# Padding SBUF slots by 32 bytes in a one-core decoder block (hybrid HGRN2 and sliding-window attention)

## The chip, the cores and the metric

One core of a Trainium2 chip runs the whole program. The metric is the device time of one execution in microseconds (us), the median of several. TensorE multiplies a stationary operand (the weights, loaded by an instruction of their own, LDWEIGHTS) with a moving operand (512 token columns at most); its granted clock has two levels, 1.2 and 2.4 GHz. In the profile PE is TensorE's matmul row, PEld its weight loads, DVE VectorE, ACT ScalarE, POOL GpSimd, SP SyncE.

## The reference, cut to what matters

One layer of a decoder block, on 512 tokens of width 2048, all in float32:

```
h = modulate(rms_norm(x, norm1_g), shift1, scale1)
proj = h @ w_in                       # 2048 -> 9728: HGRN2 q,f,i,g | attention q,k,v | two gates
o_hg = HGRN2 recurrence, chunkwise    # 8 heads of 128
o_at = sliding-window attention       # 16 heads of 64, window 128, sinks, relative bias
merged = sigmoid(gate_hg) * (o_hg @ w_branch_hg) + sigmoid(gate_at) * (o_at @ w_branch_attn)
x = x + gate1 * (merged @ w_out)
h2 = modulate(rms_norm(x, norm2_g), shift2, scale2)
x = x + gate2 * (square(relu(h2 @ w_ff1)) @ w_ff2)
```

The conditioning (shift, scale, gate) comes from another product, silu(c) @ w_ada.

## The kernel before, in words

All activations lie transposed, 128 channels on partitions by 512 tokens. A projection makes one tile of 128 output channels at a time: for each block of 128 input channels it multiplies a 128x128 piece of weights with the 512 token columns. To keep float32 accuracy with the faster one-pass float32r products, weights and activations are each split into a high part and a low part, and each block takes three products (function mm3): high weights times high activations, high weights times low activations, low weights times high activations. Each of the three is preceded by its own weight load, so the stream on TensorE is load, product, load, product, and the load for the next product runs while the present one streams.

The main stream is a list of items; an item is a piece of weights of 128 x 512 (four blocks, twelve products). Raw weights arrive by DMA from SP's queue into `raw` slots (3 of 4096 bytes a partition). `pump_splits` runs up to two items ahead: ScalarE copies a piece into a `whi` slot, VectorE writes the remainder into a `wlo` slot (4 slots each). The moving tiles come in pairs of neighbouring slots, high and low: `A` slots (32) hold the 16 pairs of the normalized input (later those of the merged branches and of the second norm), `O` slots (25) hold among others the eight pairs of a branch's output or of an eighth of the MLP's hidden layer, and in the first 190 us raw conditioning weights that DMAs write there. A planner in Python orders the side work (attention, HGRN2, conditioning) between the main products; its costs are constants and know nothing of addresses.

All these slots are 2048 bytes a partition, and come from one pool that lays tags out in the order of their first use: C, T, O, L, then 8 small slots `s` of 32 bytes and one `s16` of 64, then raw, whi, wlo, A and the rest. So within one tag all slots begin at the same offset modulo 2048; whi, wlo and A begin at one and the same offset, and O begins 320 bytes lower (8 x 32 + 64), which is 192 modulo 512. The 16 KB at the beginning of each partition are scratch for the descriptors of DMAs that GpSimd issues; after it and the slots some hundred bytes are left of the partition.

```
def mm3(ps, whi, wlo, x, first, last):
    mm(ps, whi, x[0], first, False)
    mm(ps, whi, x[1], False, False)
    mm(ps, wlo, x[0], False, last)
...
def take(tag, shape=None, dt=F32, name=None):
    pl.live[tag] = pl.live.get(tag, 0) + 1
    return act.tile(shape or [P, T], dt, tag=tag, bufs=BUFS[tag], name=nm(name or tag))
```

Of the kernel before, what the change touches and what calls it, by code (L numbers as in the profile page):

```python
# [11 lines left out]
F32R = mybir.dt.float32r  # L12
# [5 lines left out]
P = 128  # L18
T = 512
# [15 lines left out]
BUFS = {"A": 32, "O": 25, "C": 16, "T": 6, "L": 5, "ada": 3, "raw": 3, "whi": 4, "wlo": 4}  # L35


class Plan:
    """Keeps an estimate of each engine's time, and interleaves side work with the main stream of products."""

    def __init__(self):
        self.clk = {"PE": 0.0, "DVE": 0.0, "ACT": 0.0}
# [44 lines left out]
def tile_block(ctx, tc, xT, cT, wada1, wada2, badaT, g1T, g2T, wg0, win, wbat, wbhg, wout, wfg, wff1, wff2,  # L87
               lbT, hggT, qgT, kgT, sinks, table, ident_d, mask_d, onehot_d, neg_d, outT):
    nc = tc.nc
# [4 lines left out]
    act = ctx.enter_context(tc.tile_pool(name="act", bufs=1))  # L94
# [6 lines left out]
    def nm(s):  # L101
        uid[0] += 1
        return f"{s}_{uid[0]}"
# [4 lines left out]
            n *= s  # L108
        return n

# [1 line left out]
    def tt(out, in0, in1, op):  # L112
        nc.vector.tensor_tensor(out=out, in0=in0, in1=in1, op=op)  # L113
        pl.op("DVE", free_size(out) * 1.04 + 70)

    def stt(out, in0, scalar, in1, op0, op1):
        nc.vector.scalar_tensor_tensor(out=out, in0=in0, scalar=scalar, in1=in1, op0=op0, op1=op1)  # L117
        pl.op("DVE", free_size(out) * 1.04 + 70)

    def ts(out, in0, s1, op0, s2=None, op1=None):  # L120
        if op1 is None:
            nc.vector.tensor_scalar(out=out, in0=in0, scalar1=s1, scalar2=None, op0=op0)
        else:
            nc.vector.tensor_scalar(out=out, in0=in0, scalar1=s1, scalar2=s2, op0=op0, op1=op1)
        pl.op("DVE", free_size(out) * 0.6 + 70)
# [28 lines left out]
        PE.transpose(out=out, in_=in_, identity=ident)  # L154
        pl.op("PE", 107)

# [1 line left out]
    def take(tag, shape=None, dt=F32, name=None):  # L158
        pl.live[tag] = pl.live.get(tag, 0) + 1
        return act.tile(shape or [P, T], dt, tag=tag, bufs=BUFS[tag], name=nm(name or tag))  # L160

    def drop(tag, n=1):
# [17 lines left out]
    def small(n=4):  # L180
        return act.tile([P, n], F32, tag="s", bufs=8, name=nm("s"))

# [1 line left out]
    def cload(name, shape, src, dt=F32):  # L184
        t = cst.tile(shape, dt, name=name)
        G.dma_start(out=t, in_=src)
        return t
# [3 lines left out]
    for kt in range(KT):  # L191
        t = take("C")
# [18 lines left out]
    eps = cst.tile([P, 1], F32, name="eps")  # L211
# [3 lines left out]
    one = ones[:, 0:1]  # L215
# [20 lines left out]
    tt(c_act, c_sb, csig, ALU.mult)  # L236
    G.dma_start(out=cdram, in_=c_act)

# [1 line left out]
    def split(src, hi, lo):  # L240
        sact(hi, src, AF.Copy)
        tt(lo, src, hi.bitcast(F32), ALU.subtract)
# [4 lines left out]
        mm(ps, wlo, x[0], False, last)  # L247

    def newton(ps, s, y, w):
        """y * (1.5 - 0.5 (s ps + eps) y^2), with w = y^2."""  # L250
        stt(w, ps, EPS / s, w, ALU.add, ALU.mult)
        ts(w, w, -0.5 * s, ALU.mult, 1.5, ALU.add)
        tt(y, y, w, ALU.mult)
# [9 lines left out]
        for _ in gen:  # L263
            pass

# [1 line left out]
    items = []  # L267
    loads = []

    def add_load(src, n):  # L270
        loads.append((src, n))
        return len(loads) - 1
# [2 lines left out]
        items.append((ld, c0, w, emit, pre, post))  # L275

    def add_tile(srcs, xs, post, pre=None):
        """One tile of 128 output channels; xs() gives the (hi, lo) tiles of the moving side."""
        cell = {}
        nk = 8 * len(srcs)  # L280
        for hf, src in enumerate(srcs):
            ld = add_load(src, 1024)
            for q in range(2):
                k0 = hf * 8 + q * 4

                def emit(hi, lo, k0=k0):
                    x = xs(k0 + 4)
                    if k0 == 0:
                        cell["ps"] = acc()
                    for k in range(4):  # L290
                        mm3(cell["ps"], hi[:, k * P:(k + 1) * P], lo[:, k * P:(k + 1) * P], x[k0 + k], k0 + k == 0,
                            k0 + k == nk - 1)
                        if k == 1:
                            pl.drive()

                end = k0 + 4 == nk
                add_item(ld, q * T, T, emit, pre if k0 == 0 else None, (lambda: post(cell["ps"])) if end else None)
# [24 lines left out]
    def pump_splits(upto):  # L322
        while state["split"] < min(upto + 1, len(items)):
            ld, c0, w, *_ = items[state["split"]]
            hi = act.tile([P, w], F32R, tag="whi", bufs=BUFS["whi"], name=nm("whi"))
            lo = act.tile([P, w], F32R, tag="wlo", bufs=BUFS["wlo"], name=nm("wlo"))
            split(raws[ld][:, c0:c0 + w], hi, lo)
            wts[state["split"]] = (hi, lo)
            state["split"] += 1
# [13 lines left out]
        if drive:  # L343
            pl.drive()

# [1 line left out]
    def ada_step(a, raw, kt):  # L347
        if kt == 0:
            ts(a, raw, c_act[:, 0:1], ALU.mult)
# [8 lines left out]
        return act.tile([P, T], F32, tag="aa", bufs=1, name=nm("aa"))  # L358

    def ada_rest():  # L360
        """The other four parts: output channels on partitions, a quarter of the inputs at a time."""
        n = 0
        raw = []

        def fetch(n):
            while len(raw) < min(n + BUFS["ada"], 256):
                t = act.tile([P, T], F32, tag="ada", bufs=BUFS["ada"], name=nm("ada"))
                SP.dma_start(out=t, in_=wada2[len(raw)])
                raw.append(t)

        fetch(0)
        for g in range(4):
            for q in range(4):
                cb = ada_acc()
                SP.dma_start(out=cb, in_=bass.AP(cd.tensor, cd.offset + T * q, [[0, P], [1, T]]))
                lead = state["item"] + 2
                while state["item"] < lead:
                    yield "wait"
                for i in range(16):
                    fetch(n)  # L380
                    while state["item"] < n_start + PACE * n or 0 < len(mg) < KT:
                        yield "wait"
                    t = raw[n]
                    nc.vector.scalar_tensor_tensor(out=t, in0=t, scalar=1.0, in1=cb, op0=ALU.mult, op1=ALU.mult,  # L384
                                                   accum_out=adaq[:, i, q:q + 1])
                    pl.op("DVE", 680)
                    n += 1
                    yield
            d = slice(32 + 16 * g, 48 + 16 * g)
            t = adaq[:, :, 0]  # L390
            for q in range(1, 4):
                tt(t, t, adaq[:, :, q], ALU.add)
            tt(adaT[:, d], t, adaT[:, d], ALU.add)
            yield

# [1 line left out]
    h = []  # L397
    ev = {}

# [19 lines left out]
    sums = {}  # L419

    def start_evac(i, j, ps):
        """Tile i's products with the channel tiles 2j and 2j + 1 join its sum."""
        last = j == KT // 2 - 1
        key = skeys[i]
        if i in HELD:
            if not last:
                return
            src = ps
        else:
            if j == 0:  # L430
                sums[i] = take("O")
                sact(sums[i], ps, AF.Copy)
            else:
                tt(sums[i], ps, sums[i], ALU.add)
            drop("mx")
            src = sums[i]
        if last:
            if i < len(akeys):
                if i in HELD:
                    evac_to(key, "O", AF.Copy)(src)  # L440
                else:
                    ev[key] = src
                return
            if key[0] in ("q", "g"):
                evac_silu(key, "C")(src)
            else:
                evac_to(key, "C", AF.Copy if key[0] == "v" else AF.Sigmoid)(src)
            if i in HELD[NACC:]:
                drop("mx")
            elif i not in HELD:  # L450
                drop("O")
# [32 lines left out]
    for hd in range(NH):  # L484
# [3 lines left out]
        for kk in ("f", "q", "v", "g"):  # L488
            key = (kk, hd)
# [7 lines left out]
                add_tile(next_win(), hx, evac_silu(key, "C"))  # L497
    n_mix = len(items)

    # branches with their gates  # L500
    m = {}
    sig = {}
    xb = {0: [], 1: []}
# [63 lines left out]
                        msdone[n] = True  # L567
                add_tile([wb[n - SKEW[br]]], ready(xb[br]), post)

    # output projection  # L570
    x1 = []
    xr = {}
    sqs = {}
# [28 lines left out]
    for n in range(KT - 1):  # L602
        add_tile(halves(wout, n), ready(mg), out_post(n), xload(n))

    # the last tile of the projection and the first products of the MLP go by halves of the tokens,
    # so that the norm of one half runs under the products of the other
    HALF = [slice(0, T // 2), slice(T // 2, T)]
    h2 = []
    kept = []
# [168 lines left out]
    for g in range(8):  # L778
        for i in range(8):
            n = 8 * g + i  # L780
# [4 lines left out]
            add_tile([wff2[g, n]], ready(a_t[g]), ff2_post(g, n))  # L785
        items[a0 + 1], items[a0 + 2] = items[a0 + 2], items[a0 + 1]

# [1 line left out]
    def make_lb():  # L789
        mxl = small(8)  # L790
        tt(mxl, lbl[:, 0, :], lbl[:, 1, :], ALU.max)
# [126 lines left out]
        drop("T")  # L918
        drop("L")

# [1 line left out]
    oat = []  # L922

    def k_norm(raw):
# [50 lines left out]
        out.append(y)  # L975

    def att_unit(c, n, i, st):
        """Queries of block n: two heads of each of the chunk's two key heads, one in each half of the array."""
        qn, kn, vn, rq, bias, o = st["q"], st["k"], st["vn"], st["rq"][0], st["bias"], st["o"]
        rows = [slice(0, 64), slice(64, 128)]  # L980
        w = 128 if n == 0 else 256
# [47 lines left out]
        for half in range(nh):  # L1029
            t = take("L")  # L1030
# [67 lines left out]
        if c == 1:  # L1098
            yield from split_raw(oat, xb[0])

# [1 line left out]
    ohg = []  # L1102
    hgc = {}

# [167 lines left out]
        if hd == NH - 1:  # L1272
            drop("C", 3)

# [1 line left out]
    ctx.enter_context(tc.manual_schedule())  # L1276
    startup()
    assert state["item"] == n_start
# [104 lines left out]
```

## Time and profile before

| what | us |
|---|---|
| median of three runs | 2794.94 |
| lowest and highest of them | 2793.41, 3927.64 |
| span of the profiled execution | 2793.4 |
| PE busy in it (12630 products) | 2770.4 |
| DVE busy | 1305.8 |
| ACT busy | 932.3 |
| DMA queue of SP, share of 16 engines | 38.9% |

The profiled execution has a span of 2793.4 us, equal to the lowest run's 2793.41: nothing measurable lies around the span, and the median stands 1.5 us above it. Products are pipelined and overlap, so a product's own duration in the trace (about 390 ns) is not its cost; its cost is the distance from its start to the next one's start, called pace below.

### The profile page before, as it was taken

The numbers are of one execution on the slowest core, as the hardware profiler recorded it, in microseconds if no ns is written. First come the engines' busy times: TensorE is split into PE (matmuls) and PEld (weight loads), VectorE is DVE, ScalarE is ACT, GpSimd is POOL, SyncE is SP. The second block draws the span as 40 slices with busy tenths as digits, with TensorE's granted clock in tenths as the row PEclk, the third lists the DMA queues.
The fourth block names the chain that finished last, engine by engine and source line by source line (L and its number), as shares of the span: only waits on it lengthen the run. The fifth ranks groups of instructions, "written<-read, shape, count | busy, mean of one in ns | idle before, by whom it ended". The sixth has DMA issues, their size and how long they took to land.

```text
span 2793.4 us, 33013 instructions
## 1 busy us (share of the span) xinstructions
PE 2770.4 (99%) x12630; PEld 2225.1 (80%) x12630; DVE 1305.8 (47%) x2574; ACT 932.3 (33%) x1686; POOL 14.6 (1%) x28
## 2 busy tenths in 40 slices
PE   8999999999999999999999999999999999999999
PEld 4777777888888888888888888888888888888887
DVE  4778787655444555565543333233333323323333
ACT  4244455453222322232342332323323223232231
POOL 1000000000000000000000000000000000000000
PEclk9999999999999999999999999999999999999999
DMA  8852322434555555555223222222222222222233
GB/s 316 290 185 90 125 84 80 148 124 153 192 183 185 185 188 181 171 185 186 96 90 106 98 91 91 98 98 93 98 96 93 96 98 98 92 97 97 93 109 109
DMA packets 133791, 369.50 MB, mean 132 GB/s; under 512 B 15169, under 2 KB 15297, under 8 KB 133633
## 3 DMA queue, kind: packets, MB, share of 16 engines
q1 hardware_dynamic: 132480, 364.96, 38.9%
q0 software_dynamic: 1152, 2.43, 0.3%
q8 instruction: 99, 1.62, 0.3%
q14 instruction: 60, 0.48, 0.0%
HBM read 363.11 MB, written 4.23 MB: 131 GB/s over the span
## 4 chain that ended last, share of the span: by engine, by line
PE 97%; DVE 2%; ACT 1%; DMA 0%; issue 0%; SPq 0%; ACTq 0%
PE acc L150 87%; PE mx L150 9%; PE mx L154 1%; DMA C<-xT 0%; DVE wlo L113 0%; SPq L193 0%; DVE T L117 0%; DVE L L117 0%; DVE T L113 0%; ACT A L146 0%; ACT T L146 0%; ACT whi L146 0%; DVE s L999 0%; DVE C L117 0%; DVE A L117 0%
## 5 line engine op out<-in xcount | busy, mean ns | idle before, releaser
L150 PE MATMUL acc<-A,whi 128*128 128x512 f32 (+1 forms) x4608 | 1422.6, 390 | 2.5 <-ACT A L146 1.9
L150 PEld LDWEIGHTS acc<-A,whi 128*128 128x128 f32 x4608 | 858.1, 188 | 193.0 <-issue 9.0
L150 PE MATMUL acc<-A,wlo 128*128 128x512 f32 (+1 forms) x2304 | 894.7, 388 | 1.4 <-DVE wlo L113 1.4
L146 ACT ACTIVATE whi<-raw 128x512 fp32r<-128x512 f32 x944 | 570.0, 626 | 944.1 <-PE acc L150 879.1
L150 PE MATMUL acc<-O,whi 128*128 128x512 f32 x2560 | 803.0, 394 | 0.0
L113 DVE TENSOR_TENSOR wlo<-raw,whi 128x512 fp32r<-128x512 f32 x944 | 625.9, 686 | 357.1 <-ACT whi L146 355.6
L150 PEld LDWEIGHTS acc<-O,whi 128*128 128x128 f32 x2560 | 478.8, 187 | 118.1
L150 PEld LDWEIGHTS acc<-A,wlo 128*128 128x128 f32 x2304 | 433.1, 188 | 92.2 <-DVE wlo L113 2.2
L150 PE MATMUL acc<-O,wlo 128*128 128x512 f32 x1280 | 504.3, 394 | 0.0
L117 DVE SCALAR_TENSOR_TENSOR C<-acc,adaT,C 128x512 f32<-128x512 f32 x128 | 96.1, 751 | 453.0 <-PE acc L150 453.0
L150 PEld LDWEIGHTS acc<-O,wlo 128*128 128x128 f32 x1280 | 239.4, 187 | 59.2
L113 DVE TENSOR_TENSOR O<-T,O 128x512 fp32r<-128x512 f32 x64 | 44.4, 693 | 381.8 <-ACT O L146 381.8
L146 ACT ACTIVATE T<-acc 128x512 f32<-128x512 f32 x92 | 55.1, 598 | 460.3 <-PE acc L150 460.3
L384 DVE SCALAR_TENSOR_TENSOR ada<-ada,aa 128x512 f32<-128x512 f32 x256 | 175.6, 687 | 37.4 <-DMA ada<-wada 32.8
L150 PE MATMUL mx<-A,whi 128*128 128x512 f32 (+1 forms) x448 | 135.6, 385 | 2.4 <-ACT A L146 2.0
L150 PEld LDWEIGHTS mx<-A,whi 128*128 128x128 f32 x448 | 83.0, 193 | 24.2 <-issue 5.0
L150 PE MATMUL mx<-A,wlo 128*128 128x512 f32 (+1 forms) x224 | 84.9, 379 | 0.0
L146 ACT ACTIVATE T<-T 128x512 f32<-128x512 f32 (+1 forms) x102 | 62.6, 622 | 6.0 <-DVE T L113 3.4
L146 ACT ACTIVATE T<-C 128x512 f32<-128x512 f32 (+1 forms) x33 | 20.2, 617 | 94.9 <-DVE C L117 89.9
L150 PEld LDWEIGHTS mx<-A,wlo 128*128 128x128 f32 x224 | 43.2, 193 | 7.9
L113 DVE TENSOR_TENSOR O<-mx,O 128x512 f32<-128x512 f32 x56 | 37.9, 687 | 16.8 <-PE mx L150 15.8
L146 ACT ACTIVATE C<-acc 128x512 f32<-128x512 f32 x26 | 15.5, 598 | 86.7 <-PE acc L150 86.6
(155 smaller groups left out, 979.7 us busy)
## 6 DMA issues: line engine op xcount, KB each, us to landing
raw<-wff SPq DMA_DIRECT2D x248, 512.0 KB, 3.3
raw<-win SPq DMA_DIRECT2D x128, 512.0 KB, 3.7
ada<-wada SPq DMA_DIRECT2D x256, 256.0 KB, 4.0
O<-wada SPq DMA_DIRECT2D x128, 256.0 KB, 5.3
raw<-wout SPq DMA_DIRECT2D x32, 512.0 KB, 3.8
raw<-wg SPq DMA_DIRECT2D x24, 512.0 KB, 4.6
raw<-wbat SPq DMA_DIRECT2D x16, 512.0 KB, 3.4
raw<-wbhg SPq DMA_DIRECT2D x16, 512.0 KB, 3.5
```

Source lines behind the costliest of these rows:

```text
L113: nc.vector.tensor_tensor(out=out, in0=in0, in1=in1, op=op)
L117: nc.vector.scalar_tensor_tensor(out=out, in0=in0, scalar=scalar, in1=in1, op0=op0, op1=op1)
L146: nc.scalar.activation(out=out, in_=in_, func=func, **kw)
L150: PE.matmul(out, lhsT=lhsT, rhs=rhs, start=start, stop=stop)
L154: PE.transpose(out=out, in_=in_, identity=ident)
L384: nc.vector.scalar_tensor_tensor(out=t, in0=t, scalar=1.0, in1=cb, op0=ALU.mult, op1=ALU.mult, accum_out=adaq[:, i, q:q + 1])
```

## The change

Slots of `A`, `O`, `whi` and `wlo` become 2080 bytes instead of 2048; the tile used is the first 2048 bytes of its slot. Successive slots thus begin 32 bytes further on modulo 512. That needs 57 x 32 + 8 x 32 = 2080 bytes more a partition, for which the descriptor scratch of GpSimd's DMAs goes from its default of 16384 to 8192 bytes. Beside this, comments and docstrings are removed. No instruction is added or taken away.

```diff
     def take(tag, shape=None, dt=F32, name=None):
         pl.live[tag] = pl.live.get(tag, 0) + 1
+        if tag in ("A", "O"):
+            t = act.tile([P, T + 8], dt, tag=tag, bufs=BUFS[tag], name=nm(name or tag))[:, 0:T]
+            return t if shape is None else t.rearrange("p (a b) -> p a b", a=shape[1])
         return act.tile(shape or [P, T], dt, tag=tag, bufs=BUFS[tag], name=nm(name or tag))
...
-            hi = act.tile([P, w], F32R, tag="whi", bufs=BUFS["whi"], name=nm("whi"))
-            lo = act.tile([P, w], F32R, tag="wlo", bufs=BUFS["wlo"], name=nm("wlo"))
+            hi = act.tile([P, w + 8], F32R, tag="whi", bufs=BUFS["whi"], name=nm("whi"))[:, 0:w]
+            lo = act.tile([P, w + 8], F32R, tag="wlo", bufs=BUFS["wlo"], name=nm("wlo"))[:, 0:w]
...
-    nc = _bacc.Bacc("TRN2", target_bir_lowering=False, num_devices=1)
+    nc = _bacc.Bacc("TRN2", target_bir_lowering=False, num_devices=1, dynamic_dma_scratch_size=8192)
```

## Rows read from the trace of the kernel before

**Rows 1.** The page: engines' busy time and the granted clock in 40 slices

```profile
PE 2770.4 (99%) x12630; PEld 2225.1 (80%) x12630; DVE 1305.8 (47%) x2574; ACT 932.3 (33%) x1686; POOL 14.6 (1%) x28
...
PEclk9999999999999999999999999999999999999999
```

**Rows 2.** Waits of PE, longest first (total us, times, longest us)

```profile
PE mx L150 <- DVE T L113: 9.8, 4, 6.5
```

**Rows 3.** The chain that ended last (start us, us, what)

```profile
1419.96 1369.75 PE acc L150 x5952
```

**Rows 4.** The page's costliest groups: main products (count, busy us, mean ns)

```profile
L150 PE MATMUL acc<-A,whi 128*128 128x512 f32 (+1 forms) x4608 | 1422.6, 390 | 2.5 <-ACT A L146 1.9
...
L150 PE MATMUL acc<-A,wlo 128*128 128x512 f32 (+1 forms) x2304 | 894.7, 388 | 1.4 <-DVE wlo L113 1.4
...
L150 PE MATMUL acc<-O,whi 128*128 128x512 f32 x2560 | 803.0, 394 | 0.0
...
L150 PE MATMUL acc<-O,wlo 128*128 128x512 f32 x1280 | 504.3, 394 | 0.0
...
L150 PE MATMUL mx<-A,whi 128*128 128x512 f32 (+1 forms) x448 | 135.6, 385 | 2.4 <-ACT A L146 2.0
...
L150 PE MATMUL mx<-A,wlo 128*128 128x512 f32 (+1 forms) x224 | 84.9, 379 | 0.0
```

**Rows 5.** Timeline of PE, moving tiles A, settled (start us, us, instruction)

```profile
1342.18 0.39 PE L150 MATMUL acc<-A,wlo 128*128 128x512 f32 x1
...
1356.46 0.39 PE L150 MATMUL acc<-A,wlo 128*128 128x512 f32 x1
```

**Rows 6.** Timeline of PE, moving tiles O, settled

```profile
2000.06 0.39 PE L150 MATMUL acc<-O,wlo 128*128 128x512 f32 x1
...
2007.06 0.39 PE L150 MATMUL acc<-O,wlo 128*128 128x512 f32 x1
```

**Rows 7.** Timeline of PE, products of 256 columns, full clock

```profile
1357.29 0.28 PE L150 MATMUL acc<-A,wlo 128*128 128x256 f32 x1
...
1359.09 0.28 PE L150 MATMUL acc<-A,wlo 128*128 128x256 f32 x1
```

**Rows 8.** Timeline of PE, products of 256 columns, half clock

```profile
1378.41 0.42 PE L150 MATMUL mx<-A,wlo 128*128 128x256 f32 x1
...
1380.97 0.41 PE L150 MATMUL mx<-A,wlo 128*128 128x256 f32 x1
```

**Rows 9.** Windows: engines' busy time (count), granted clock, DMA share, GB/s

```profile
1502.00:1549.00 47.00, 47.00 (x203) 37.64 (x203) 17.08 (x27) 10.74 (x17) 0.00 (x0) 1.00 0.27 90
...
1378.60:1381.20 2.60, 2.60 (x15) 2.60 (x14) 1.60 (x4) 0.90 (x2) 0.00 (x0) 0.50 0.22 88
```

**Rows 10.** Timelines of PE, the change from moving tiles O to A

```profile
1552.92 0.62 PE L150 MATMUL acc<-A,whi 128*128 128x512 f32 x2
1553.38 0.39 PE L150 MATMUL acc<-A,wlo 128*128 128x512 f32 x1
...
1554.30 0.62 PE L150 MATMUL acc<-A,whi 128*128 128x512 f32 x2
...
1553.14 0.40 PE L150 MATMUL acc<-A,whi 128*128 128x512 f32 x1
```

**Rows 11.** Timeline of POOL: transfers it issues (idle before, releaser)

```profile
8.39 0.54 POOL L186 DMA_DIRECT2D lbl<-lbT  x1 [0.80 <-DMA tab_sb<-table]
...
28.89 0.51 POOL L811 DMA_DIRECT2D rv<-T  x1 [17.73 <-DVE T L113]
...
166.56 3.00 POOL L1058 DMA_DIRECT2D O<-rv  x4 [72.25 <-DVE aa L117]
```

## The prediction

> **What bounds the kernel now.** I read the page first: PE is busy 99% of the span at full granted clock in every slice, and DVE, the next engine, 47% [rows 1]. The waits then say how little PE stands still: the largest sum is 9.8 us, at the start [rows 2]. The chain of work that ended last is PE's own sequence: from 1419.96 us to the end it is 5952 products in 1369.75 us, 230.1 ns each, with no other engine in it [rows 3]. So the time is the number of products times their pace, and a change that adds and removes no instruction can only act through the pace.
>
> The page's groups give the numbers [rows 4]: with moving tiles A 4608 + 2304 + 448 + 224 = 7584 products (a few of them, the second form, of 256 columns); with O 2560 + 1280 = 3840. Together 11,424.
>
> The paces come from timelines, between two starts far apart. A: 21 groups of three products from 1342.18 to 1356.46 us, 14.28 us / 63 = 226.7 ns [rows 5]. O: 10 groups from 2000.06 to 2007.06, 7.00 / 30 = 233.3 ns [rows 6]. 512 columns at one per cycle of the granted 2.4 GHz would be 213.3 ns. So there is an excess, 13.3 ns with A and 20.0 ns with O. In total 7584 x 13.3 + 3840 x 20.0 = 101 + 77 = 178 us, 15.6 ns a product in the mean. That is all that the change could win, and the reader is to ask what the excess hangs on:
> - Not on columns: 256-column products go at 1.80 us / 15 = 120.0 ns [rows 7], and 256 columns take 106.7, so the excess is 13.3 again. It belongs to a weight load or a change of weights, once per product.
> - It is gone at half clock: 12 products in 2.56 us, 213.3 ns [rows 8], with the granted clock at 0.50 [rows 9]; 256 columns at 1.2 GHz are 213.3. A moving stream at half its rate leaves the load room. This speaks for two reads that TensorE makes at once, the columns and the next weights, getting into each other's way.
> - It differs between A and O, which differ in their offset to the weight slots (0 against 192 modulo 512) and keep it for all slots. This speaks for an influence of offsets. Two values are known; the change replaces them by a mixture.
> - It is probably not the writes of other engines or the DMAs: in a stretch at O's pace DVE is busy 17.08 of 47.00 us, ACT 10.74, DMA 27% [rows 9], and starts keep a fixed distance through it.
>
> **The change part by part.** *Longer A, O, whi and wlo slots.* Slot i now begins 32 x i bytes further modulo 512 than before. During a product with moving slot i, the load for the next product reads a weight slot j, so the distance between both goes through all 16 multiples of 32: the 32 A slots and the four weight slots cover them evenly, O's 16 slots of a branch nearly so. The new pace is the mean over 16 offsets instead of the pace of one. Only two are priced: offset 0, 226.7 ns, and offset 192, 233.3 ns. From below the bound is 213.3 ns (no excess at any offset), from above the slowest step that the trace shows. That is in the change from O to A: the settled pace of A doesn't come at once. The first six products with A, from 1552.92 to 1554.30 us, take 1.38 us, 230.0 ns each, and the second of them runs from 1553.14 to 1553.38, which is 0.24 us [rows 10]; the pair that starts at 1552.92 lasts 0.46 us, so with 226.7 for the first the second takes 233 to 240 ns. I take 236. So at the same offset the excess also depends on how the two streams happened to start, and a fixed offset lets them settle into a rhythm; with a new offset at every product there may be none.
>
> Value taken: 230.0 ns for all. It is the plain mean of the two settled paces, and it is also what A does while unsettled, so two different rows lead to it. A: (230.0 - 226.7) x 7584 = +25.3 us. O: (230.0 - 233.3) x 3840 = -12.8 us. Sum +12.5 us on the span of 2793.4, hence 2806; the median of the runs stood 1.5 us above the span, hence 2807. Bounds: -178 us, and with 236 ns 9.3 x 7584 + 2.7 x 3840 = +81 us.
>
> Here a rule of the Trainium skill speaks against any effect. "TensorE: Matmul & The Clock Gate", in "Step-by-step: what each phase is for", says that TensorE has two independent SBUF read ports, one for the moving operand and one for weight loads, so that loading the next weights takes no read bandwidth from the running product. By it offsets could not matter and the time would stay at 2795. The trace does not fit the rule's consequence well: an excess of 13.3 or 20.0 ns stands beside every load at full clock. But no row shows directly that the load causes it, so the rule keeps a chance below.
>
> *Writes by ScalarE, VectorE and DMAs into shifted slots.* Same lengths, same number of instructions; nothing on the chain. DVE would have to more than double to bind (47%) [rows 1]: 0.
>
> *Descriptor scratch halved.* POOL issues 24 transfers. In the first 12 us it already waits up to 0.80 us for an earlier transfer before it issues the next; if halving made each of the 14 first ones wait so, 11.2 us, that ends inside the 17.73 us in which POOL idles before the next one [rows 11]. The four bias tables at 166.56 us are issued in 3.00 us; if each had to wait for the one before, attention starts some us later, and the main products cover that, since PE had other work there. I cost it at 0; without that cover it would be under 15 us, once.
>
> *Removed comments*: nothing.
>
> **The rivals.**
> *Faster: most offsets are free.* If only some distances collide, 0 and 192 happen to be two of them. For: the excess depends on the offset at all, and before, every product sits on one of two offsets. Against: both of the offsets that the trace shows cost, neither is zero, and columns pass much more memory than 512 bytes during one load, so a shift of the start should change when they meet rather than whether. If half of the 16 offsets are free and the others cost the mean of the known two, 16.7, the mean excess is 8.3 instead of 15.6: 7.2 x 11,424 = -83 us, 2712. If only the known two cost, 2.1 ns remain and the time is 2641. The gain passes 2% from six free offsets on.
>
> *Slower: the rhythm is lost.* Each product meets another distance than the one before, and the streams never settle; each costs what the second product after a change of tiles costs, 236 ns: 2793 + 81 + 1.5 = 2876. For: rows 10. Against: in the same rows the mean over the unsettled six is only 230.0. It decides from about 234 ns on (+56 us).
>
> *Nothing: offsets don't matter.* A and O would differ for another reason, and both paces stay: 2795. For: the rule above, and the exact constancy of both paces. Against: no other difference between A and O products is visible; both have the same shapes, weights and accumulators.
>
> The page has a formula that gives another time: the section "Back-to-back issue gap" states N / 2.4 + 2.5 ns, 215.8 for 512 columns, as the warm gap. By it the rest of the excess would be removable, and the change would give 2644 if it removed it. The rows differ from it (226.7 and 233.3), so it serves here as the far end of the first rival only, with no chance beyond that.
>
> **How the numbers follow.** Forecast, a mixture with about the same mean: 0.46. Nothing: 0.16. Both lie within 2% (56 us, about what a measurement of this kernel can tell from no change): together 0.62. Faster by over 2%: 0.22. Slower by over 2%: 0.16. The likeliest case's time is 2807; its own range, with paces of 226.7 to 233.3 for all products, is 2793 - (6.7 x 3840 = 26) to 2793 + (6.7 x 7584 = 51), or 2767 to 2845. The range to hold 8 in 10 reaches to the half-free case at 2712 and to 2860, short of the full loss of rhythm; some 0.1 is left out on either side.
>
> **What the profile after would show.** If the forecast holds: the chain still ends in some 5950 products in a row, now at 228 to 232 ns in the mean; the settled 0.68 us of three A products is replaced by distances that vary from product to product and repeat with the slots; half-clock products still go at 213.3 ns. If offsets don't matter, 0.68 and 0.70 us for three products come back unchanged. If the first rival holds, many single distances of 0.21 us appear, and then other work may come into view: the first 680 us, where attention and HGRN2 lie beside the products, would not shrink in proportion. The prediction is wrong above all if the mean over offsets isn't near the two known ones; no row prices the other 14.

## The result and the profile after

The median after is 2819.12 us (2817.78 to 2819.78, four runs) against 2794.86 for the kernel before with one run more than shown above: a ratio of 1.0089, 95% interval 1.0074 to 1.0104. The one run of the kernel before that took 3927.64 us stands 40% above the others and is left out of the ratio. The kernel became slower by 24.3 us, less than the 2% that the bounds of the chances ask for; the forecast of +12.5 us has the direction and half of the size. The profiled execution has a span of 2817.7 us, also 24.3 more than before.

The page after first: busy time (share, instructions) of the engines, the granted clock, and the first group of products with either moving tile.

```profile
PE 2795.8 (99%) x12630; PEld 2228.0 (79%) x12630; DVE 1306.3 (46%) x2574; ACT 932.1 (33%) x1686; POOL 14.5 (1%) x28
...
PEclk9999999999999999999999999999999999999999
...
L150 PE MATMUL acc<-A,whi 128*128 128x512 f32 (+1 forms) x4608 | 1440.5, 394 | 2.7 <-ACT A L146 1.9
...
L150 PE MATMUL acc<-O,whi 128*128 128x512 f32 x2560 | 801.7, 394 | 0.0
```

PE's busy time rose by 25.4 us [rows 1], those of DVE, ACT and POOL stayed within 0.5 us, the counts are the same, the clock too. The two groups differed by 4 ns in the mean of one, 390 and 394 [rows 4]; now both have 394. So A's products lost (1422.6 to 1440.5 us in this group) and O's gained little (803.0 to 801.7). As durations overlap, the sizes are taken from the starts below.

The longest waits of PE after (us in total, times, longest) and the chain that ended last (start, length, what):

```profile
PE mx L150 <- DVE T L113: 8.7, 5, 6.7
```

```profile
684.01 694.50 PE acc L150 x3030
...
1435.09 1378.95 PE acc L150 x5952
```

The waits are smaller than before, if anything [rows 2]. The chain still ends in 5952 products in a row, now 1378.95 us long instead of 1369.75 [rows 3], 231.7 ns each. The 3030 products ahead of them take 694.50 us; in the chain of before they took 686.20, from 677.92 on:

```profile
677.92 686.20 PE acc L150 x3030
```

This splits the loss by place: 684.01 - 677.92 = 6.1 us up to the first of these stretches, 8.3 in it, 0.7 between, 9.2 in the last: 24.3. The loss is spread over the products and sits in no single place.

By tiles it splits with the starts of stretches. In the MLP 384 products with O and 384 with A take turns; the timeline of PE after shows the first product of each stretch (start us, us, instruction):

```profile
1746.52 0.39 PE L150 MATMUL acc<-A,whi 128*128 128x512 f32 x1
...
1835.32 0.40 PE L150 MATMUL acc<-O,whi 128*128 128x512 f32 x1
...
1924.37 0.40 PE L150 MATMUL acc<-A,whi 128*128 128x512 f32 x1
...
2013.17 0.40 PE L150 MATMUL acc<-O,whi 128*128 128x512 f32 x1
```

A: 1835.32 - 1746.52 = 88.80 us, and again 2013.17 - 1924.37 = 88.80; divided by 384, 231.25 ns, where the settled pace was 226.7 [rows 5]. O: 89.05 us, 231.9 ns; over the seven O stretches of the MLP that end in an A stretch the mean is 89.14, 232.1 ns, against 233.3 [rows 6]. Inside this last A stretch the single paces now lie between 226 and 236 ns by the trace's starts, where a settled A stretch of before has 226 and 227 throughout. Over groups of three this nearly evens out; the next rows are the starts of the last product of such groups.

```profile
2006.00 0.39 PE L150 MATMUL acc<-A,wlo 128*128 128x512 f32 x1
...
2006.70 0.39 PE L150 MATMUL acc<-A,wlo 128*128 128x512 f32 x1
...
2007.39 0.39 PE L150 MATMUL acc<-A,wlo 128*128 128x512 f32 x1
...
2012.93 0.40 PE L150 MATMUL acc<-A,wlo 128*128 128x512 f32 x1
```

0.70, then 0.69; ten such groups from 2006.00 to 2012.93 give 231.0 ns. At half clock nothing changed: the window (us; busy time and count of PE, PEld, DVE, ACT, POOL; granted clock; DMA share; GB/s) stands at 0.50, and nine products of 256 columns take 1.92 us, 213.3 ns each as before [rows 8].

```profile
1393.00:1395.30 2.30, 2.30 (x13) 2.30 (x12) 1.32 (x4) 0.88 (x2) 0.00 (x0) 0.50 0.27 110
```

```profile
1392.87 0.41 PE L150 MATMUL mx<-A,wlo 128*128 128x256 f32 x1
...
1394.79 0.41 PE L150 MATMUL mx<-A,wlo 128*128 128x256 f32 x1
```

The halved scratch shows on POOL (in brackets the idle time before, and the releaser): in the first 12 us it waits five times instead of three for an earlier transfer, none longer than 0.71 us, and lbl is issued at 8.70 us instead of 8.39 [rows 11]; before the next transfer POOL idles 16.70 us.

```profile
8.70 0.53 POOL L189 DMA_DIRECT2D lbl<-lbT  x1 [0.41 <-DMA tab_sb<-table]
...
28.35 0.51 POOL L814 DMA_DIRECT2D rv<-T  x1 [16.70 <-DVE T L113]
```

### The profile page after: what moved, and what is told of

Its sections match the earlier page's. It is cut to its first block, busy times and chain, and to the rows that moved or that the text cites. A ratio compares the mean times of both kernels' runs of the same rounds, so it can differ in the third digit from the quotient of the medians.

```text
span 2817.7 us, 33013 instructions
## 1 busy us (share of the span) xinstructions
PE 2795.8 (99%) x12630; PEld 2228.0 (79%) x12630; DVE 1306.3 (46%) x2574; ACT 932.1 (33%) x1686; POOL 14.5 (1%) x28
## 4 chain that ended last, share of the span: by engine, by line
PE 97%; DVE 1%; ACT 0%; DMA 0%; issue 0%; SPq 0%; ACTq 0%
PE acc L150 87%; PE mx L150 9%; PE mx L154 1%; DMA C<-xT 0%; DVE wlo L113 0%; DVE T L113 0%; DVE L L117 0%; ACT T L146 0%; DVE s L1002 0%; SPq L196 0%; DVE C L117 0%; DVE T L117 0%; DVE C L124 0%; DVE s L113 0%; ACT whi L146 0%
## 5 line engine op out<-in xcount | busy, mean ns | idle before, releaser
L150 PE MATMUL acc<-A,whi 128*128 128x512 f32 (+1 forms) x4608 | 1440.5, 394 | 2.7 <-ACT A L146 1.9
L150 PE MATMUL acc<-O,whi 128*128 128x512 f32 x2560 | 801.7, 394 | 0.0
```

What stands on the lines that cost most here:

```text
L150: PE.matmul(out, lhsT=lhsT, rhs=rhs, start=start, stop=stop)
```

## The experiments

Diffs are against the kernel before; of the two kernels of products alone (1 and 5) only the series are shown. All variants of the block have the scratch at 8192 bytes. "Distance" is the start of the moving tile less the start of the weight tile, in bytes. A kernel "settles" at a pace when the starts keep it to the end of the series or stretch.

**1. Each distance by itself.** A kernel of products alone: series of 96, same shapes and types, the distance set by slices, held through a series.

```diff
+    def x(b):
+        e = b // 4
+        return lambda i: (xb if i % 3 == 1 else xa)[:, e:e + T]
+    for b in range(0, 512, 32):
+        arm(f"b{b:03d}", x(b), w)
```

> This kernel computes none of the block: it runs 27 series of 96 products (128x128 weights, 512 columns, float32r, a weight load before each) on tiles at chosen offsets, and stores what comes out. 19 series hold the distance between moving tile and weights fixed (0 to 480 bytes in steps of 32, and 4, 8, 16), two change it at every product (named mixed and step), three load fewer weight columns (half0, quarter0, half192), one uses 2-byte operands (bf). Theory S (settling): at a fixed distance the pace settles within some six products at a value of its own between 213 and 236 ns, 226.7 at distance 0 and 233.3 at 192, and the two series that change it stay near 231.5, the pace after the change. Theory M (mixture): every distance has its own pace, the 16 differ, and their plain mean is 231.5; then mixed and step are just that mean. Theory F (free offsets): some distances go at 213.3 ns. If the weight load's reads are the cause, half the weight columns cost about half the excess (6.7 ns at 0), a quarter about 3.3, and 2-byte operands little (under 3 ns).

Measured: the first product of series 0, 32, 64 and so on to 256, and of the one after, in PE's timeline:

```profile
30.09 0.39 PE L55 MATMUL b<-xa,wa 128*128 128x512 f32 x1
...
51.85 0.40 PE L55 MATMUL b<-xa,wa 128*128 128x512 f32 x1
...
74.25 0.40 PE L55 MATMUL b<-xa,wa 128*128 128x512 f32 x1
...
96.23 0.40 PE L55 MATMUL b<-xa,wa 128*128 128x512 f32 x1
...
118.64 0.40 PE L55 MATMUL b<-xa,wa 128*128 128x512 f32 x1
...
141.04 0.40 PE L55 MATMUL b<-xa,wa 128*128 128x512 f32 x1
...
163.53 0.39 PE L55 MATMUL b<-xa,wa 128*128 128x512 f32 x1
...
185.92 0.40 PE L55 MATMUL b<-xa,wa 128*128 128x512 f32 x1
...
208.31 0.40 PE L55 MATMUL b<-xa,wa 128*128 128x512 f32 x1
...
230.07 0.40 PE L55 MATMUL b<-xa,wa 128*128 128x512 f32 x1
```

The differences, 21.76, 22.40, 21.98, 22.41, 22.40, 22.49, 22.39, 22.39 and again 21.76 us, divided by 96, are the paces: 226.7 ns at 0, 233.3 at 32, 229 at 64, 233.3 at 96 and 128, 234.3 at 160, 233.3 at 192 and 224, and 226.7 at 256. From there the same eight values come again up to 480. So the pace repeats every 256 bytes; the paces of before, 226.7 at 0 and 233.3 at 192, come back without the block around them; and 0 is the best of the eight, not a middle one. The mean of the eight is 232.1. The chain of the same kernel has the other series:

```profile
454.06 22.09 PE half L55 x96
476.15 22.25 PE quarter L55 x96
498.40 22.34 PE half L55 x96
...
541.47 22.25 PE mixed L55 x96
563.72 22.48 PE step L55 x96
```

A series with the distance changed at random from product to product ("mixed") goes at 22.25 / 96 = 231.8 ns, one with a step of 32 bytes each time at 234.2. So theory F falls, and theory M holds for the mixed series but misses the step by 2 ns. Loading 64 or 32 weight columns instead of 128 at distance 0 doesn't lower the pace but raises it, to 230.1 and 231.8; at distance 192, loading 64 (the second "half" row) gives 232.7 against 233.3. The excess is thus not simply the bytes of the weight load.

**2. The scratch alone.**

```diff
-    nc = _bacc.Bacc("TRN2", target_bir_lowering=False, num_devices=1)
+    nc = _bacc.Bacc("TRN2", target_bir_lowering=False, num_devices=1, dynamic_dma_scratch_size=8192)
```

> The kernel before with the descriptor scratch halved and nothing else. Theory: 2795 within 2 us, since POOL's few transfers are hidden. Rival, that part of the loss comes from the scratch: 2800 to 2819.

2794.20 us, ratio 1.0000 (0.9991 to 1.0009). Its chain ends in a row that repeats [rows 3] to 0.02 us. The scratch costs nothing.

```profile
1419.94 1369.75 PE acc L150 x5952
```

**3. One distance for all.** No padding; an unused tile of 192 bytes after the small slots moves raw, whi, wlo and A, so that O too stands at distance 0 (modulo 512).

```diff
+        gap = act.tile([P, 48], F32, tag="gap", bufs=1, name=nm("gap"))
+        nc.vector.memset(gap, 0.0)
```

> The kernel before with the scratch halved and one unused tile of 192 bytes laid between the O and the raw slots, so that O tiles, like A tiles, begin at distance 0 (modulo 512) from the weight slots. If the fixed distance sets the settled pace, O products go at 226.7 instead of 233.3 ns: 3840 x 6.67 = 25.6 us less, 2769. If A and O differ for another reason than their offset, 2795.

2767.72 us, ratio 0.9906 (0.9891 to 0.9921): faster than both kernels. The chain, and the first products of an O stretch, of the A stretch behind it and of the next O stretch:

```profile
677.01 680.50 PE acc L150 x3030
...
1413.36 1349.13 PE acc L150 x5952
```

```profile
1630.79 0.39 PE L150 MATMUL acc<-O,whi 128*128 128x512 f32 x1
...
1717.83 0.39 PE L150 MATMUL acc<-A,whi 128*128 128x512 f32 x1
...
1804.87 0.39 PE L150 MATMUL acc<-O,whi 128*128 128x512 f32 x1
```

Both stretches last 87.04 us: 226.7 ns for O as for A. The instructions of O's products are those of before. By the order of the tags O, which is laid out ahead of the unused tile, didn't move; the weights did, and A with them, whose pace stayed. So it is the distance that counts and not the place of either tile. The gain, 1369.75 - 1349.13 = 20.6 us in the last part, is 6.7 ns for each of its 3072 products with O.

**4. Half of the change: the weight slots alone.**

```diff
-            hi = act.tile([P, w], F32R, tag="whi", bufs=BUFS["whi"], name=nm("whi"))
+            hi = act.tile([P, w + 8], F32R, tag="whi", bufs=BUFS["whi"], name=nm("whi"))[:, 0:w]
```

(and the same for lo)

> Only the whi and wlo slots are 2080 bytes, A and O keep 2048 (scratch halved). Within an item of twelve products the distance then stays fixed and changes only from item to item among four values. Theory S: the streams settle inside each item after some five products, so about half of the products go at a settled pace and half at about 231: 2795 to 2812. Theory M: each distance has its pace at once and the time is the mean of four of them for A and four for O, for which only 0 and 192 are known; anything from 2770 to 2830, and distances can be told apart by item in the trace.

2826.67 us, ratio 1.0118 (1.0101 to 1.0135). To the whi slots A's distances become 0, -32, -64 and -96, O's 192, 160, 128 and 96. The wlo slots lie behind the four longer whi slots and so 4 x 32 = 128 bytes further on, A another 128: to them A's distances are 128, 96, 64 and 32, O's 64, 32, 0 and -32. The first products of an A, an O and an A stretch:

```profile
1571.35 0.39 PE L150 MATMUL acc<-A,whi 128*128 128x512 f32 x1
...
1660.58 0.39 PE L150 MATMUL acc<-O,whi 128*128 128x512 f32 x1
...
1749.81 0.39 PE L150 MATMUL acc<-A,whi 128*128 128x512 f32 x1
```

89.23 us for both, 232.4 ns. Of the three loads of a group two are of whi, one of wlo; with these weights the means of experiment 1 over the distances are 232.0 for A and 232.6 for O. Here a mean of single paces is good to 0.4 ns, some 5 us of this kernel; for the whole change, with its distances that change from product to product, it is 232.1 against 231.25 and 232.1 measured. What a product costs depends on the order of the distances as well (experiment 5).

**5. Finer distances, pairs of distances, other operands.** Products alone again, series of 48: all distances from 0 to 252 in steps of 4; pairs in which every third product has a moving tile at another distance ("p0x64": 0, and 64 for the third); operands of two bytes; fewer columns.

```diff
+    for b in range(0, 256, 4):
+        arm(f"f{b:03d}", x(b), w)
+    for b0, b1 in ((0, 0), (0, 64), (0, 128), (0, 192), (64, 0), (128, 0), (192, 0), (0, 32), (32, 0)):
+        arm(f"p{b0}x{b1}", x2(b0, b1), w)
+    for b in (0, 16, 32, 96):
+        arm(f"bf{b}", lambda i, b=b: xbf[:, b // 2:b // 2 + T], lambda i: wbf[:, 128 * (i % 4):128 * (i % 4) + 128])
```

> Again none of the block is computed: series of 48 products as in the first such run. 64 series hold distances of 0 to 252 bytes in steps of 4; nine give the two moving tiles of a triple different distances (p0x128: the high tile at 0, the low one at 128); four have 2-byte operands at 0, 16, 32 and 96; six have 256 or 128 columns at 0, 32 and 128. Theory: the pace depends on the distance modulo 256, 0 is the lowest or nearly so, and 2-byte operands stay at 216 ns at every distance, since only the 4-byte stream at full clock collides. Rival, that a better distance exists between the multiples of 32: some series under 226 ns. For the pairs: if each product pays for its own distance alone, p0x128 costs (2 x 226.7 + 233.3) / 3 = 228.9; if the changing itself costs, more than that. Fewer columns: the excess per product stays (120.0 for 256 columns at 0, 126.7 at 32).

The chain (series that follow each other merge when the digits of their names alone differ):

```profile
20.39 715.27 PE f L55 x3072
735.66 44.22 PE p0x L55 x192
...
790.96 10.98 PE p128x L55 x48
801.94 11.24 PE p192x L55 x48
...
835.40 0.23 PE bf L55
...
876.85 17.10 PE c256x L88 x144
```

The 64 fine distances go at 715.27 / 3072 = 232.8 ns in the mean. In the timeline none settles below 226.7, which besides 0 is reached at six others (28, 60, 156, 236, 240 and 252); the slowest settle at 240.0 (20, 132, 196 and 244). There is no better place than 0 to be found. With two-byte operands the distance makes no difference: four series from 835.40 to 876.85, 41.45 us / 192 = 215.9 ns. Products of 256 columns turned against what was expected: they settle at 120.0 ns at distance 0 but at 117.8 at 32 and 118.7 at 128 (17.10 / 144 = 118.8 for the three), so which distance is good depends on the length as well. Products of 128 columns settle at 111.7 ns at all three. The four "p0x" pairs together take 230.3 ns; the one with 128 for the third product settles at 233.3, where the paces of its parts would give (226.7 x 2 + 233.3) / 3 = 228.9. But the reverse, two at 128 and the third at 0 ("p128x"), goes at 10.98 / 48 = 228.8 where its parts would give 231.1, and "p192x" at 234.2 against 231.1. So the order of the distances counts, and a change can cost or save.

**6. The other half: the moving slots alone.**

```diff
     def take(tag, shape=None, dt=F32, name=None):
+        if tag in ("A", "O"):
+            t = act.tile([P, T + 8], dt, tag=tag, bufs=BUFS[tag], name=nm(name or tag))[:, 0:T]
+            return t if shape is None else t.rearrange("p (a b) -> p a b", a=shape[1])
```

> Only the A and O slots are 2080 bytes, whi and wlo keep 2048 (scratch halved). Successive products then differ in distance just as in the whole change: 2819 within 5 us by both theories, since the distances run through all multiples of 32 either way. If the two kinds of padding added up (24 and 32 us), the other half would be missing here and the time would be near 2790.

2823.90 us, ratio 1.0108 (1.0093 to 1.0123). Either half alone costs as much as the whole or a little more (ratios 1.0118 and 1.0108 against 1.0089, with intervals that overlap): the halves don't add up, since each is enough to take A off its distance.

**7. A moved to a worse distance, still without padding.** An unused tile of 160 bytes ahead of A.

```diff
+                gap = act.tile([P, 40], F32, tag="gap", bufs=1, name=nm("gap"))
+                nc.vector.memset(gap, 0.0)
```

> No slot is padded; one unused tile of 160 bytes lies between wlo and A (scratch halved), so that A stands at the fixed distance 160, the slowest of the 16 in the series run (234.3 ns), and O stays at 192. If the distance alone sets the pace, A products cost 234.3 instead of 226.7 ns: 7584 x 7.6 = 58 us more, 2852, worse than the whole change though nothing changes from product to product. If a fixed distance always settles to a good pace in the kernel, 2795.

2844.41 us, ratio 1.0182 (1.0165 to 1.0199). The first products of an A, an O and an A stretch:

```profile
1580.58 0.39 PE L150 MATMUL acc<-A,whi 128*128 128x512 f32 x1
...
1670.54 0.40 PE L150 MATMUL acc<-O,whi 128*128 128x512 f32 x1
...
1760.15 0.39 PE L150 MATMUL acc<-A,whi 128*128 128x512 f32 x1
```

A: 89.96 us, 234.3 ns, the value of 160 in experiment 1; O: 89.61, 233.4, the pace of before within 0.1. Where products run in long stretches at one distance the pace is that of the series within 0.1 ns. The 58 us that were expected came to 50.8, since the short stretches of the first part lose less (below); the last part pays in full, 1391.57 - 1369.75 = 21.8 us or 7.6 ns for each of its 2880 products with A:

```profile
1446.16 1391.57 PE acc L150 x5952
```

**8. The period.** Weight slots longer by 256 bytes instead of 32.

```diff
-            hi = act.tile([P, w], F32R, tag="whi", bufs=BUFS["whi"], name=nm("whi"))
+            hi = act.tile([P, w + 64], F32R, tag="whi", bufs=BUFS["whi"], name=nm("whi"))[:, 0:w]
```

(and the same for lo)

> As the run in which only the weight slots are longer, but by 256 bytes instead of 32, so that slots begin at different offsets that are equal modulo 256 (scratch halved). If the pace depends on the distance modulo 256, as the series run showed, A stays at 0 and O at 192 for every slot: 2794, against 2827 with 32 bytes. If changing slots' offsets costs whatever the step, 2815 to 2830.

2794.29 us, ratio 1.0000 (0.9990 to 1.0009). Longer slots are harmless as such; with distances equal modulo 256 the time is that of before.

```profile
1419.32 1369.75 PE acc L150 x5952
```

## Why the prediction was right and wrong

*The bound* held: all of the loss is PE's own pace, the waits didn't grow, the chain has the shape that was foretold.

*The mechanism* held: an influence of the distance between moving tile and weights, A losing and O gaining by a mixture. Experiments 3 and 7 show the influence with no padding at all, experiment 1 with nothing else in the kernel, and experiment 8 shows that longer slots do nothing as long as the distance stays.

*The step that failed* is the value taken, 230.0 ns for all, the plain mean of the two settled paces. The runs show 231.5 in its place (231.25 with A, 232.1 with O, weighted by their counts), since the mean over all distances is 232.1. Product by product: A forecast at +25.3 us; the stretches show 231.25 - 226.7 = 4.55 ns, times 7584 = +34.5 for settled stretches. O forecast at -12.8; the stretches show 233.3 - 232.1 = 1.2 ns, times 3840 = -4.6. Sum +29.9, of which 24.3 arrived. The last 5952 products bear the terms out: they hold 2880 with A and 3072 with O, 13.1 - 3.7 = 9.4 us, and the chain shows 9.2. Most of the 5.6 us that are missing belong to the first 678 us (6.1 us where 4.55 ns for each of the 2167 products with A there would be 9.9). A's products there had not settled before either, as in [rows 10], and so had less to lose. The chains show it, the first two rows from before, the other two the same pieces after:

```profile
219.74 4.13 PE acc L150 x18
...
575.46 20.47 PE acc L150 x90
```

```profile
221.88 4.17 PE acc L150 x18
...
580.22 20.81 PE acc L150 x90
```

The short piece loses 0.04 us, 2.2 ns a product; the long one 0.34, 3.8 ns. From the starts of all products with A that directly follow another in this part (1969 in either trace, those with a wait left out) the mean pace goes from 228.1 to 231.3: 3.2 ns, or 6.3 us.

Two reasons led to the value, and both were weak. The mean of two known values was taken for the mean of all, where the known ones were the best and a typical one: of the eight distances five lie at 233.3, one at 234.3. And A's "unsettled" 230.0 ns was read as the pace of a mixture, though all six of these products stand at distance 0: by the trace's starts they go at 226, 236, 228, 233, 231 and 226 ns and then stay at 226.7, a passage between two settled paces that says nothing of other distances.

*The period* was taken as 512 bytes; it is 256. This changed nothing in the sum, since sixteen multiples of 32 cover both. *An excess once per product whatever the columns* was read at distance 0 alone and doesn't hold elsewhere: over one column per cycle it is 20.0 ns at distance 32 with 512 columns, 11.1 with 256 (experiment 5). No term rested on it. The upper end of the likeliest case's own range, 2793 + 51, is 2844 and not 2845.

*The scratch at nothing* was right (experiment 2), and so was its cover: POOL's waits for an earlier transfer grew from three to five and vanished in the 17 us in which it idles.

*Rivals.* "Most offsets are free" fell: none of the 64 distances tried goes below 226.7 ns. "The rhythm is lost", 236 ns, fell in its price, but its idea is half true: the order of the distances counts (p0x128 costs 4.4 ns more than its parts, p128x0 2.3 less), and a mixture with a step of 32 each time goes at 234.2. In the order of the changed kernel the pace is 231.7. "Nothing" fell with experiment 3. It rested on a rule: the Trainium skill, "TensorE: Matmul & The Clock Gate", section "Step-by-step: what each phase is for", has two independent read ports, by which a weight load takes nothing from the product that runs. The traces don't agree with the consequence that place is indifferent: 233.3 against 226.7 ns for the same instructions. They don't show either that the load's reads are the cause, since fewer weight columns made it slower at distance 0 and only 0.6 ns faster at 192.

*What stays open* is the physical cause: why 256 bytes, why two-byte operands are immune, why a narrower load is slower at distance 0, why the order counts, and why at half clock the excess is gone, at distance 0 [rows 8] as in the mixture after.

## What to carry to other kernels

Where the chain is one engine's own sequence, price the pace, and before spreading a layout over many cases ask whether the present case is the best of them: a mixture takes about the mean, and a small kernel of products that holds each case for a hundred repetitions tells that in one run. With float32r products of 512 columns that reload weights each time, put all moving tiles at the same offset modulo 256 bytes as the weight tiles; here 192 unused bytes gave 26 us, where the padding cost 24. With 256 columns that place was the slowest of the three tried. Two known points bound a mean only if one knows where they stand among the rest.

## What the runs showed of the hardware

- The pace of 512-column float32r products with a weight load each depends on the distance of moving and weight tile modulo 256 bytes, from 226.7 to 240.0 ns (experiments 1, 3, 5, 7 and 8); two-byte operands show none of it at the distances tried (215.9 ns).
- The Trainium skill, "TensorE: Matmul & The Clock Gate", section "Back-to-back issue gap", states N / 2.4 + 2.5 ns as the warm gap of an isolated product, 215.8 for 512 columns. The two-byte series agree with it though each product has a load before it; the four-byte products miss it by 11 ns at their best distance.
- With 256 columns distance 0 is the slowest of the three tried: 120.0 ns at 0, 117.8 at 32, 118.7 at 128. With 128 columns all three go at 111.7.
- Loading 32 of 128 weight columns at distance 0 made the products slower, 231.8 against 226.7 ns.
